# One ring of four banks for the GLA mixer's values, updates and outputs, and the output's transposes moved behind the second value

## The chip, the cores and the metric

The kernel runs on one core of one Trainium2 chip. The metric is the device time of one execution in microseconds (us), as the median of several runs. Three runs of the kernel before took 2820.91, 2823.19 and 2827.33 us.

Names used below: PE is TensorE's matmuls and PEld its weight loads, DVE is VectorE, ACT is ScalarE, POOL is GpSimd, SP is SyncE, which issues the DMAs. PSUM is the memory that matmuls write to; it has eight banks, and the stage of this change uses all eight.

## The reference

One step of a two-layer trunk on 1024 prompt frames and 32 frames of a running stream, model width 1024. Layer 0 mixes with retention, layer 1 with gated linear attention (GLA); behind each mixer stands a convolutional feed-forward part. The change concerns GLA: 4 heads, keys of 128, values of 256.

```python
def gla_chunk(S, xs):
    q, k, v, lg = xs
    b = jnp.cumsum(lg, axis=1)
    expo = b[:, :, None] - b[:, None, :]          # masked to be causal
    A = jnp.einsum('bihd,bjhd,bijhd->bhij', q, k, jnp.exp(expo))
    intra = jnp.einsum('bhij,bjhe->bihe', A, v)
    cross = jnp.einsum('bihd,bhde->bihe', q * jnp.exp(b), S)
    S_new = jnp.exp(bL)[..., None] * S + jnp.einsum('bjhd,bjhe->bhde', k * jnp.exp(bL[:, None] - b), v)
    return S_new, intra + cross
...
    o = o * lax.rsqrt(jnp.mean(o * o, axis=-1, keepdims=True) + EPS) * norm_g
    return (jax.nn.silu(r) * o) @ w_out, S
```

A frame's output is the scores A times the values, plus the decayed query times the state S; then the state is decayed and updated with keys times values. The output of each head is normalised over its 256 columns.

## The kernel before

All matmuls are fp32 by parts: each operand is split into a high part and a remainder (names ending in h and l), and three products are added in PSUM (high x high, high x low, low x high).

The 1056 frames are cut into three chunks c of 384, 384 and 288 columns, and each chunk into minors of 128 frames (the last minor of chunk 2 is the 32 sample frames). The GLA stage (`gla`, L891) runs over twelve units, one for each head h and chunk c. For a unit the code is written in this order:

- `project` of the *next* unit: gate, query and key, 49 matmuls into two banks called "pj".
- `store[0]`, that is `finish` of the *previous* unit: its last minor's `attend`, then the normalisation: DVE and ACT turn the sums of squares into a factor (L1157 to L1162) and DVE scales the output tile `oraw` (L1164).
- `scores` of this unit: many small matmuls into two banks "lv" (L1005, L1011, L1023), DVE masks (L1015, L1028) that build A, transposes of the decayed keys kd into "pj" (L1036), then the splits of A and of the keys on ACT and DVE (L1044 to L1048).
- `store[1]` of the previous unit: for each half e of the 256 output columns three transposes of `oraw` (L1170) into a bank of "pj" (e = 0) or "lv" (e = 1), one copy on ACT (L1173) and one DMA to DRAM (L1174). Only the next layer part reads it.
- `mix` of this unit: `value(0)`, `value(1)`, `attend(0)`, `value(2)`, `attend(1)`.
- `weigh` of the next unit: differences on POOL (L968, L972), exponentials on ACT (L1188) and products on DVE (L970, L974) for seven levels of the decay.

A `value` is 24 matmuls of 128x256 into a bank of tag "v" (two of them), read by ACT (vh, L1102) and DVE (vl, L1103). For the sample frames it is 16 matmuls, with vh from L259 and L260. An `attend` first splits the state (gSh on ACT L1077, gSl on DVE L1078). Then come three matmuls for the update `pu` (L1119 to L1121), read by DVE at L1124, which makes the new state gS, and six for the output `po` (L1135 to L1141), read twice by ACT: the squares (L1142) and the copy to `oraw` (L1143). `pu` and `po` share the tag "ou" with two banks.

This written order is not the order on the chip. A planner at compile time puts the instructions of each engine in one fixed queue: of those that its own costs say are ready, the one that was written earliest goes first. It also gives each tile a bank of its tag's ring. On the chip each engine works through its queue in order, and an instruction that comes to a bank that has not been read out yet waits, with all that stands behind it. So matmuls of the first value stand among the scores and the transposes today, wherever the planner held the latter not ready.

Of the kernel before, what the change touches and what calls it, by code (L numbers as in the profile page):

```python
# [9 lines left out]
F32 = mybir.dt.float32  # L10
# [6 lines left out]
P = 128  # L17
# [11 lines left out]
GH, GDK, GDV = 4, 128, 256  # L29
# [23 lines left out]
def trunk_kernel(ctx: ExitStack, tc: tile.TileContext, io):  # L53
# [3 lines left out]
    def pool(name, bufs=1, **kw):  # L57
        return tc.tile_pool(name=name, bufs=bufs, reuse_waits="tile", **kw)
# [30 lines left out]
    def uid():  # L89
        cnt[0] += 1  # L90
        return cnt[0]
# [799 lines left out]
    def gla(closers):  # L891
# [3 lines left out]
        pp = es.enter_context(pool("gps", space=PSUM))  # L895
# [8 lines left out]
        def t384(pl, tag, dt=F32, bufs=2, w=384):  # L904
            return pl.tile([P, w], dt, tag=tag, name=f"{tag}_{uid()}", bufs=bufs)
# [3 lines left out]
        def groups_of(c):  # L909
            return [(0, 3, P)] if c < 2 else [(0, 2, P), (2, 3, TS)]  # L910
# [142 lines left out]
        state = {}  # L1053
        mask = [None]

        def mix(h, c, u):
            Ah, Al, qh, ql, kh, kl, eL = u
            c0, n = CM[c]
            mins = minors(c)
            groups = groups_of(c)  # L1060
            if c == 0:
                wv[h] = [load_w(io["w_gv"][h, t]) for t in range(2)]
                if h == GH - 1:
                    preload(("w_gg", 0), ("w_gg", 1))
                state[h] = None
            if (h, c) == units[-1]:
                oraw = w_tile(f"oraw{uid()}").bitcast(F32)[:, :3 * GDV].rearrange(
                    "p (m e) -> p m e", m=3)
            else:
                oraw = g2.tile([P, 3, GDV], F32, tag="oraw", name=f"oraw{uid()}", bufs=2)  # L1070
            ss = g2.tile([P, 3, 4], F32, tag="gss", name=f"gss{uid()}", bufs=2)
            vs = {}

            def split_state(st, tag):
                sh = g2.tile([P, GDV], F32R, tag=f"gSh{tag}", name=f"gSh{uid()}", bufs=1 if tag else 2)
                sl = g2.tile([P, GDV], F32R, tag=f"gSl{tag}", name=f"gSl{uid()}", bufs=1)
                S.copy(sh, st)  # L1077
                V.tensor_tensor(sl, st, sh.bitcast(F32), op=ALU.subtract)  # L1078
                return sh, sl

            if c == 2:
                st = g2.tile([P, GDV], F32, tag="gSi", name=f"gS{uid()}")
                nc.sync.dma_start(st, io["state_gla"][h])
                s_in = st, *split_state(st, "i")

            def value(mi):
                o, t0, L = mins[mi]
                m = t0 // P
                pv = pp.tile([P, GDV], F32, tag="v", name=f"pv{uid()}", bufs=2)

                def wpart(kt):
                    ev = slice((kt % 4) * GDV, (kt % 4) * GDV + GDV)
                    return [w_[:, ev] for w_ in wv[h][kt // 4]]

                value_rows(pv, wpart, t0, xs)
                vh = g2.tile([P, GDV], F32R, tag="vh", name=f"vh{uid()}", bufs=3)
                if t0 >= TP:
                    stack_v(vh, pv)
                    vs[mi] = vh, None
                    return  # L1100
                vl = g2.tile([P, GDV], F32R, tag="vl", name=f"vl{uid()}", bufs=3)
                S.activation(vh, pv, AF.Copy, scale=rc[:, m:m + 1])  # L1102
                V.scalar_tensor_tensor(vl, pv, rc[:, m:m + 1], vh.bitcast(F32),  # L1103
                                       op0=ALU.mult, op1=ALU.subtract)
                vs[mi] = vh, vl

            def attend(mi):
                o, t0, L = mins[mi]
                vh, vl = vs[mi]
                samp = t0 >= TP  # L1110
                st = s_in[0] if samp else state[h]
                cross = st is not None
                if cross:
                    sh, sl = s_in[1:] if samp else split_state(st, "")
                pu = pp.tile([P, GDV], F32, tag="ou", name=f"ouu{uid()}", bufs=2)
                if samp:
                    PE.matmul(pu, kh[:, mi], vh, start=True, stop=True)
                else:
                    PE.matmul(pu, kh[:, mi], vh, start=True, stop=False)  # L1119
                    PE.matmul(pu, kl[:, mi], vh, start=False, stop=False)  # L1120
                    PE.matmul(pu, kh[:, mi], vl, start=False, stop=True)  # L1121
                sn = g2.tile([P, GDV], F32, tag="gS", name=f"gS{uid()}", bufs=2)
                if cross:
                    V.scalar_tensor_tensor(sn, st, eL[:, mi:mi + 1], pu, op0=ALU.mult, op1=ALU.add)  # L1124
                else:
                    S.copy(sn, pu)
                state[h] = sn
                if t0 >= TP - P:
                    dst = io["o_gla_s"] if samp else io["o_gla_p"]
                    nc.sync.dma_start(dst[h], sn)  # L1130
                po = pp.tile([P, GDV], F32, tag="ou", name=f"ou{uid()}", bufs=2)
                if samp:
                    PE.matmul(po[:L], Ah[:, mi, :L], vh, start=True, stop=False)
                else:
                    PE.matmul(po, Ah[:, mi], vh, start=True, stop=False)  # L1135
                    PE.matmul(po, Al[:, mi], vh, start=False, stop=False)
                    PE.matmul(po, Ah[:, mi], vl, start=False, stop=not cross)
                if cross:
                    PE.matmul(po[:L], qh[:, o:o + L], sh, start=False, stop=False)
                    PE.matmul(po[:L], ql[:, o:o + L], sh, start=False, stop=False)  # L1140
                    PE.matmul(po[:L], qh[:, o:o + L], sl, start=False, stop=True)  # L1141
                S.activation(oraw[:L, mi], po[:L], AF.Square, accum_out=ss[:L, mi, 0:1])  # L1142
                S.copy(oraw[:L, mi], po[:L])  # L1143

            value(0)
            value(1)
            attend(0)
            value(2)
            attend(1)

            def finish():
                attend(2)
                for m0, m1, L in groups:
                    m_ = ss[:L, m0:m1, 1]
                    r_ = ss[:L, m0:m1, 2]
                    t_ = ss[:L, m0:m1, 3]
                    V.tensor_scalar(m_, ss[:L, m0:m1, 0], 1.0 / GDV, EPS, op0=ALU.mult, op1=ALU.add)  # L1157
                    expln(t_, m_, AF.Ln)
                    expln(r_, t_, AF.Exp, scale=-0.5)
                    V.tensor_tensor(t_, r_, r_, op=ALU.mult)  # L1160
                    V.scalar_tensor_tensor(t_, t_, -0.5, m_, op0=ALU.mult, op1=ALU.mult)
                    V.scalar_tensor_tensor(r_, t_, 1.5, r_, op0=ALU.add, op1=ALU.mult)  # L1162
                    for mi in range(m0, m1):
                        V.tensor_scalar(oraw[:L, mi], oraw[:L, mi], ss[:L, mi, 2:3], None, op0=ALU.mult)  # L1164

            def store(lv, room):
                for e in range(2):
                    pt = (lv("pt") if lv else small() if e else t384(pp, "pj", w=512))[:, :3 * P].rearrange("p (m i) -> p m i", m=3)
                    for mi, (o, t0, L) in enumerate(mins):
                        PE.transpose(pt[:, mi, :L], oraw[:L, mi, e * P:e * P + P], ident[:L, :L])  # L1170
                    ot = room()
                    w = n if lv or e == 0 else 3 * P
                    S.copy(ot[:, :w], pt.rearrange("p m i -> p (m i)")[:, :w])  # L1173
                    nc.sync.dma_start(scr_o[1][2 * h + e, :, c0:c0 + n], ot[:, :n])  # L1174
            return finish, store
# [16 lines left out]
        g2 = es.enter_context(pool("g2", side="right"))  # L1192
# [22 lines left out]
        store = None  # L1215
        for i, u in enumerate(units):
            nxt = units[i + 1] if i + 1 < len(units) else None
            if nxt:
                p = project(*nxt)
            if store:  # L1220
                store[0]()
            sc = scores(*u, w)
            if store:
                store[1](None, lambda: t384(g2, "ot"))
            h, c = u
            if c == 1 and h + 1 < GH:
                for j in range(2):
                    preload(("w_gqk", h + 1, j))
                    order(last_w[1], mask[0])
            store = mix(*u, sc)  # L1230
            if nxt:
                w = weigh(*nxt, p)
        store[0]()
# [728 lines left out]
```

## Time and profile before

| | |
|---|---|
| median of three runs | 2823.19 us (2820.91 to 2827.33) |
| profiled execution, its own time | 2822.85 us |
| its span in the trace | 2820.7 us |
| TensorE matmul busy | 2748.1 us, 97% |
| VectorE, ScalarE, GpSimd busy | 74%, 47%, 10% |
| mean granted TensorE clock | 0.995 of full speed |
| the GLA units in the trace | about 1640 to 1925 us |

Times in the trace are in us from the span's start. A line of the timeline gives the start, the duration, the engine, the line of the code, the operation, the tiles (written <- read) and, in brackets, the idle time of the engine before it with what ended that. Matmuls overlap: one takes 0.28 us from start to end, and the next may start 0.12 us behind it. A list of waits gives the waiting instruction, what released it, then total us, how often, and the longest.

### The profile page before, as it was taken

The page shows a single profiled execution, that of the slowest core. Times are in us where ns is not written, and L with a number is a line of the kernel's source. Part 1 is how long each engine was busy: PE and PEld are TensorE (multiplying, and loading weights), DVE is VectorE, ACT ScalarE, POOL GpSimd, SP SyncE. Part 2 cuts the span into 40 slices and gives each one's busy share as a digit, 9 for nine tenths or more (in the row PEclk, how much of TensorE's full clock was granted, in tenths as well). Part 3 has the DMA queues.
Part 4 walks back from the last instruction along what each step waited for, and adds up shares of the span by engine and source line. Part 5 has one row for each costly group of instructions (what it writes and reads, how often), then busy time and mean ns, then how long its engine had stood idle before and what let it go on. Part 6 is the DMA issues. An engine that isn't in the chain of part 4 may idle for free.

```text
span 2820.7 us, 54472 instructions
## 1 busy us (share of the span) xinstructions
PE 2748.1 (97%) x21978; PEld 2649.3 (94%) x21978; DVE 2099.6 (74%) x3493; ACT 1322.2 (47%) x2388; POOL 273.1 (10%) x480
## 2 busy tenths in 40 slices
PE   8999999999999999999999999999999999999998
PEld 8999988878899999999999989989999999999997
DVE  7777777777577878887875687874388788878756
ACT  8433344443455544444542565653244444445434
POOL 1000000000011111111000122220021111110001
PEclk9999999999999999999999999999999999999999
DMA  6333386664866123332856511115531233328573
GB/s 223 108 121 109 107 282 204 211 194 160 273 189 219 61 84 107 137 130 84 284 194 225 186 30 53 53 45 174 170 100 62 84 107 134 134 81 284 195 237 113
DMA packets 232478, 419.48 MB, mean 149 GB/s; under 512 B 27393, under 2 KB 145793, under 8 KB 231201
## 3 DMA queue, kind: packets, MB, share of 16 engines
q1 hardware_dynamic: 231680, 415.40, 44.9%
q8 instruction: 172, 2.82, 0.4%
q14 instruction: 82, 0.66, 0.1%
q10 hardware_dynamic: 544, 0.59, 0.1%
HBM read 292.08 MB, written 123.85 MB: 147 GB/s over the span
## 4 chain that ended last, share of the span: by engine, by line
PE 80%; DVE 9%; DMA 5%; ACT 4%; issue 2%; POOL 1%; SPq 0%; DVEq 0%; ACTq 0%; POOLq 0%
PE pu L341 16%; PE pu L336 16%; PE pu L340 16%; PE pd L1316 3%; PE pd L1315 3%; PE pd L1317 3%; PE psv L242 1%; PE psv L241 1%; PE psv L240 1%; PE pj L127 1%; PE pj L128 1%; DMA raw<-w_ro 1%; PE pj L129 1%; PE pg L127 1%; PE pg L128 1%
## 5 line engine op out<-in xcount | busy, mean ns | idle before, releaser
L106 DVE TENSOR_TENSOR wlo<-raw,whi 128x1024 fp32r<-128x1024 f32 (+1 forms) x147 | 179.7, 1226 | 94.9 <-ACT whi L106 39.8
L1571 ACT COPY AR<-pu 128x264 f32<-128x264 f32 x264 | 98.8, 374 | 292.8 <-PE pu L341 290.1
L341 PE MATMUL pu<-XA,wgl 128*128 128x264 f32 x752 | 213.6, 284 | 0.0
L336 PE MATMUL pu<-XA,wgh 128*128 128x264 f32 x752 | 213.0, 283 | 0.0
L340 PE MATMUL pu<-XA,wgh 128*128 128x264 f32 x752 | 213.0, 283 | 0.0
L106 ACT CAST whi<-raw 128x1024 fp32r<-128x1024 f32 (+1 forms) x147 | 152.7, 1042 | 103.8 <-DMA raw<-w_ro 41.3
L1593 DVE SCALAR_TENSOR_TENSOR AR<-AR,cw 128x1058 f32<-128x1058 f32 x88 | 116.0, 1319 | 58.5 <-ACT AR L1592 54.0
L1315 PE MATMUL pd<-XB,whi 128*128 128x264 f32 x552 | 157.9, 286 | 1.7 <-DVE rm L212 1.7
L1317 PE MATMUL pd<-XB,wlo 128*128 128x264 f32 x552 | 157.0, 284 | 0.0
L1316 PE MATMUL pd<-XB,whi 128*128 128x264 f32 x552 | 156.7, 284 | 0.0
L336 PE MATMUL pu<-XA,wsh 128*128 128x264 f32 x520 | 148.3, 285 | 1.6 <-ACT AR L1571 0.8
L341 PE MATMUL pu<-XA,wsl 128*128 128x264 f32 x520 | 147.9, 284 | 0.8 <-DVE wsl L309 0.8
L340 PE MATMUL pu<-XA,wsh 128*128 128x264 f32 x520 | 147.2, 283 | 0.0
L1567 DVE TENSOR_TENSOR AR<-AR,pu 128x264 f32<-128x264 f32 (+2 forms) x440 | 145.1, 370 | 0.0
L309 DVE TENSOR_TENSOR wtl<-rv,wth 128x1024 fp32r<-128x1024 f32 x58 | 71.5, 1233 | 97.7 <-ACT wth L309 93.6
L336 PEld LDWEIGHTS pu<-XA,wgh 128*128 128x128 f32 x752 | 141.3, 188 | 0.0
L341 PEld LDWEIGHTS pu<-XA,wgl 128*128 128x128 f32 x752 | 141.2, 188 | 0.0
L340 PEld LDWEIGHTS pu<-XA,wgh 128*128 128x128 f32 x752 | 141.2, 188 | 0.0
L336 PE MATMUL pu<-XA,whi 128*128 128x264 f32 x448 | 127.7, 285 | 2.1 <-ACT XA L1462 1.2
L341 PE MATMUL pu<-XA,wlo 128*128 128x264 f32 x448 | 127.5, 286 | 1.5 <-DVE wlo L106 1.5
L340 PE MATMUL pu<-XA,whi 128*128 128x264 f32 x448 | 127.2, 285 | 0.5 <-DVE XA L1447 0.4
L336 PE MATMUL pu<-XA,wth 128*128 128x264 f32 x408 | 116.1, 285 | 0.7 <-ACT wth L309 0.7
(497 smaller groups left out, 10454.5 us busy)
## 6 DMA issues: line engine op xcount, KB each, us to landing
raw<-w_ro SPq DMA_DIRECT2D x52, 512.0 KB, 5.0
rg<-w_up SPq DMA_DIRECT2D x44, 512.0 KB, 3.7
rv<-w_up SPq DMA_DIRECT2D x44, 512.0 KB, 3.6
scr_h<-AR SPq DMA_DIRECT2D x44, 512.0 KB, 2.6
AR<-scr_x SPq DMA_DIRECT2D x32, 528.0 KB, 5.0
scr_x<-AR SPq DMA_DIRECT2D x32, 528.0 KB, 3.8
raw<-scr_w SPq DMA_DIRECT2D x32, 512.0 KB, 4.8
AR<-scr_h SPq DMA_DIRECT2D x28, 528.0 KB, 4.9
```

The source lines that it names most:

```text
L106: last_w[:] = S.copy(hi[:, k], raw[:, k]), V.tensor_tensor(lo[:, k], raw[:, k], hi[:, k].bitcast(F32), op=ALU.subtract)
L127: PE.matmul(ps, hi[:, k], rh, start=kt == 0, stop=False)
L309: last_w[:] = S.copy(h, src), V.tensor_tensor(l_, src, h.bitcast(F32), op=ALU.subtract)
L336: mm = PE.matmul(ps, wh[:, k], x[:, 0, kt], start=m in (1, 2, 4, 5) and kt == 0, stop=False, skip_group_check=True)
L340: PE.matmul(ps, wh[:, k], x[:, 1, kt], start=False, stop=False, skip_group_check=True)
L341: mm = PE.matmul(ps, wl[:, k], x[:, 0, kt], start=False, stop=kt == 3, skip_group_check=True)
L1315: PE.matmul(o, w[0][:, k], h[0][:, :n], start=i == 0, stop=False)
L1316: PE.matmul(o, w[0][:, k], h[1][:, :n], start=False, stop=False)
L1317: self.last_mm = PE.matmul(o, w[1][:, k], h[0][:, :n], start=False, stop=i == nk - 1)
L1567: V.tensor_tensor(u[:, d:d + n], t[:, o:o + n], b[:, o:o + n], op=op)
L1571: S.copy(t, b)
L1593: V.scalar_tensor_tensor(cj, uj[:, 1:T + 3], cw[:, nt, 1:2], cj, op0=ALU.mult, op1=ALU.add)
```

## The change

Three tile calls change their tag: the value's `pv`, the update's `pu` and the output's `po` now share one tag "vo" with four banks, in place of two tags with two banks each. In number of banks nothing changes. Each tile is asked for at the size of a full bank and cut to 256 columns.

`store[1]` of the previous unit is no longer called between `scores` and `mix`. It is handed to `mix` and called there between `value(1)` and `attend(0)`. In chunk 1 the loads of the next head's query and key weights, which are written between the two places, so come ahead of it, and in chunk 0 the loads of the value weights in `mix`. The last unit's output is transposed in the next part, as before.

```diff
-        def mix(h, c, u):
+        def mix(h, c, u, between):
...
-                pv = pp.tile([P, GDV], F32, tag="v", name=f"pv{uid()}", bufs=2)
+                pv = pp.tile([P, 512], F32, tag="vo", name=f"pv{uid()}", bufs=4)[:, :GDV]
...
-                pu = pp.tile([P, GDV], F32, tag="ou", name=f"ouu{uid()}", bufs=2)
+                pu = pp.tile([P, 512], F32, tag="vo", name=f"ouu{uid()}", bufs=4)[:, :GDV]
...
-                po = pp.tile([P, GDV], F32, tag="ou", name=f"ou{uid()}", bufs=2)
+                po = pp.tile([P, 512], F32, tag="vo", name=f"ou{uid()}", bufs=4)[:, :GDV]
...
             value(0)
             value(1)
+            if between:
+                between()
             attend(0)
             value(2)
             attend(1)
...
             sc = scores(*u, w)
-            if store:
-                store[1](None, lambda: t384(g2, "ot"))
             h, c = u
...
-            store = mix(*u, sc)
+            store = mix(*u, sc, (lambda st=store: st[1](None, lambda: t384(g2, "ot"))) if store else None)
```

## The prediction

> **What bounds the kernel now.** I read the page first.
>
> ```profile
> span 2820.7 us, 54472 instructions
> PE 2748.1 (97%) x21978; PEld 2649.3 (94%) x21978; DVE 2099.6 (74%) x3493; ACT 1322.2 (47%) x2388; POOL 273.1 (10%) x480
> ```
>
> TensorE sets the time as a whole: it is idle for 72.6 of 2820.7 us. The change touches only the GLA stage, so I then asked for the busy times of that stretch and for what TensorE waited for in it.
>
> ```profile
> 1640.00:1925.00 285.00, 270.53 (x3562) 260.07 (x3563) 222.51 (x557) 168.14 (x543) 67.50 (x83) 0.99 0.17 53
> ```
>
> Columns: stretch, its length, then busy time of PE, PEld, DVE, ACT and POOL, the granted clock, the DMA share, GB/s. TensorE is idle 14.5 us here, DVE is at 78%, ACT at 59%. Nothing else is near its limit, so what the change can win lies in these 14.5 us, in matmuls that run slower than they need, and in the clock (0.99, not 1.00).
>
> ```profile
> PE ouu L1119 <- DVE gS L1124: 3.5, 3, 1.2
> ...
> PE ou L1135 <- ACT oraw L1143: 2.0, 3, 0.7
> PE pj L1170 <- DVE oraw L1164: 1.9, 6, 0.4
> ```
>
> Three waits belong to the change, each with total, count and longest. The first two are the two-bank ring "ou": an update (pu) waits until the previous update has been added to the state, an output (po) until the previous output has been copied out. Each comes three times, in the last chunk (c = 2) of heads 0 to 2. The third is the transposes waiting for the normalised output.
>
> **The gap in chunk 2**, seen in time (head 0, instructions of PE, then ACT, then DVE):
>
> ```profile
> 1701.84 0.28 PE L246 MATMUL pv<-whi,xs 128*128 128x256 f32 x1
> 1703.31 0.36 PE L1119 MATMUL ouu<-vh,kh 128*128 128x256 f32 x1 [1.19 <-DVE gS L1124]
> 1703.51 0.28 PE L1120 MATMUL ouu<-vh,kl 128*128 128x256 f32 x1
> 1703.63 0.37 PE L1121 MATMUL ouu<-vl,kh 128*128 128x256 f32 x1
> 1704.67 0.39 PE L1135 MATMUL ou<-vh,Ah 128*128 128x256 f32 x1 [0.67 <-ACT oraw L1143]
> ```
>
> ```profile
> 1700.89 0.63 ACT L1188 ACTIVATE d<-d 128x192 f32<-128x192 f32 x2 [2.15 <-POOL d L968]
> 1702.00 0.64 ACT L1188 ACTIVATE d<-d 128x192 f32<-128x192 f32 x2 [0.47 <-POOL d L968]
> 1702.54 0.46 ACT L1102 ACTIVATE vh<-pv,rc 128x256 fp32r<-128x256 f32 x1
> ...
> 1704.24 0.37 ACT L1143 COPY oraw<-ou 128x256 f32<-128x256 f32 x1
> ```
>
> ```profile
> 1702.69 0.48 DVE L1124 SCALAR_TENSOR_TENSOR gS<-gS,eL,ouu 128x256 f32<-128x256 f32 x1
> 1703.08 0.48 DVE L1103 SCALAR_TENSOR_TENSOR vl<-pv,rc,vh 128x256 fp32r<-128x256 f32 x1
> ...
> 1703.87 0.43 DVE L1078 TENSOR_TENSOR gSl<-gS,gSh 128x256 fp32r<-128x256 f32 x1
> ```
>
> Matmuls of 128x256 that wait for nothing start 0.12 us apart (1703.51 to 1703.63). From 1701.84 to 1703.31 are 1.47 us, so 1.35 are lost before pu; from 1703.63 to 1704.67 are 1.04, so 0.92 are lost before po. ACT had been standing behind two exponentials that waited for POOL, which is why vh comes only at 1702.54.
>
> **The clock after the gap.** I laid windows over the stretches where the clock column falls:
>
> ```profile
> 1702.20:1705.62 3.42, 1.64 (x10) 1.44 (x11) 2.35 (x8) 3.21 (x10) 0.54 (x1) 1.00 0.00 0
> 1705.62:1709.03 3.41, 3.41 (x13) 3.41 (x12) 2.80 (x6) 3.41 (x10) 0.00 (x0) 0.50 0.31 61
> 1845.56:1848.98 3.42, 1.78 (x13) 1.37 (x11) 3.35 (x9) 2.74 (x10) 1.47 (x2) 1.00 0.00 0
> 1848.98:1852.39 3.41, 3.19 (x12) 3.20 (x13) 2.32 (x6) 3.41 (x9) 0.00 (x0) 0.50 0.11 12
> ...
> 1773.90:1777.30 3.40, 1.97 (x15) 1.57 (x13) 3.34 (x9) 2.69 (x10) 1.63 (x2) 1.00 0.01 2
> ```
>
> Two of the three gaps (heads 0 and 2) are followed by 3.41 us at half clock, after a stretch in which PE was busy for 1.64 and 1.78 us. Head 1's gap is as long but its busiest part fell otherwise (1.97 us) and the clock stayed. Half clock for 3.41 us costs at most 1.7 us; the second stretch has 0.2 us of idle in it, so I take 1.6 each, 3.2 in all.
>
> **The transposes.** In chunk 2 they stand together; in chunk 1 and chunk 0 they are spread among the matmuls of the first value.
>
> ```profile
> 1694.01 0.27 PE L1170 MATMUL pj<-ident,oraw 128*128 128x128 f32 x1
> ...
> 1694.58 0.36 PE L242 MATMUL pv<-whi,XA 128*128 128x256 f32 x1
> ```
>
> ```profile
> 1668.95 0.28 PE L240 MATMUL pv<-whi,XA 128*128 128x256 f32 x1
> ...
> 1670.86 0.28 PE L240 MATMUL pv<-whi,XA 128*128 128x256 f32 x1
> ```
>
> ```profile
> 1719.24 0.33 PE L1170 MATMUL pj<-ident,oraw 128*128 128x128 f32 x1
> 1719.33 0.36 PE L240 MATMUL pv<-whi,XA 128*128 128x256 f32 x1
> 1719.53 0.28 PE L241 MATMUL pv<-wlo,XA 128*128 128x256 f32 x1
> 1720.21 0.24 PE L1170 MATMUL pj<-ident,oraw 32*128 32x32 f32 x1 [0.40 <-DVE oraw L1164]
> ...
> 1720.85 0.56 PE L1170 MATMUL lv<-ident,oraw 128*128 128x128 f32 x3
> 1721.33 0.39 PE L242 MATMUL pv<-whi,XA 128*128 128x256 f32 x1
> 1721.56 0.28 PE L240 MATMUL pv<-whi,XA 128*128 128x256 f32 x1
> ```
>
> Six together take 0.57 us (1694.01 to 1694.58), 0.10 each. In chunk 1, 1.91 us hold six of them and six value matmuls: 0.60 + 0.72 = 1.32 would do, 0.59 are lost. In chunk 0, 2.32 us hold five and six (the "..." are three value matmuls): 0.50 + 0.72 = 1.22 would do, 1.10 are lost. The loss is idle time, and the slower start of a value matmul behind a transpose (0.20 instead of 0.12).
>
> **The change part by part.**
>
> No instruction is added or removed. *Transposes behind the second value* (eleven chunks; the twelfth is done in the next layer): 48 value matmuls, 5.7 us, now stand between the scores and the transposes, so the product oraw, some 0.5 us late today, is long there, and the six can stand together as in chunk 2. Worth 3 x 0.59 + 3 x 1.10 + 0, the gain where they already stand together being nothing: 5.1 us; bounds 2 (the 1.9 of the wait alone) and 6. What is late next: pu waits for kl, po for Al, but the transposes' own time still lies ahead of those. With the transposes go two copies on ACT and two stores on SP per chunk. The stores fall behind the next head's weight loads on SP; nobody in this stage reads them. The copies (0.48 us, row below) come after vh and fall into ACT's stretch before 1700.89, where 2.15 us of idle hide them; without that cover they push the exponentials and the second vh, 0.96 us in three chunks 2. I charge a third, 1.0; bounds 0 and 2.9.
>
> ```profile
> 1694.76 0.48 ACT L1173 COPY ot<-pj 128x384 f32<-128x384 f32 x1 [1.29 <-PE pj L1170]
> ```
>
> *Ring of four, po's wait.* po takes a bank that was left two tiles earlier instead of one: pu's, free at 1703.17 (gS above), before po can start at 1703.75. Its last operand gSl ends at 1704.30, and five matmuls of 0.12 cover 1703.75 to 1704.35. So 0.92 x 3 = 2.8 us; bounds 1.4 and 2.8.
>
> *Ring of four, pu's wait.* If pu's bank is free, vh still ends at 1703.00 and vl at 1703.56, and pu's third matmul needs vl: it starts at 1703.63 today. So I take 0. Lower bound: pu gets the second value's own bank and its first matmul waits for vl, 0.25 later, -0.8 in three. Upper: vh is ordered ahead of the exponentials, 1.35 x 3 = 4.0.
>
> *Clock.* Without po's 0.92 the critical stretches are busy 2.5 to 2.7 of 3.41 us, more than head 1's 1.97, which kept the clock. 3.2 us; bounds 0 and 3.2.
>
> One rule of the Trainium skill disagrees: "TensorE: Matmul & The Clock Gate", Part 1, says that the clock falls after at least one idle window of about 3.4 us. The trace has no such idle window here and the clock fell at 1.64 of 3.42 us busy, so the rows decide; by the rule the two slow stretches would have another cause and stay, and the sum would be 3.2 less.
>
> Sum: 5.1 - 1.0 + 2.8 + 0 + 3.2 = 10.1 us. The profiled execution took 2822.85 us (2.15 outside its span), 0.34 below the median 2823.19. 2822.85 - 10.1 = 2812.75; against the median **2813.1 us**.
>
> **The rivals.**
>
> *A: the gap only moves.* ACT's copies land ahead of the second vh in chunk 2 and take back 0.96 us, all of the 0.92 that po wins; the slow stretches stay. Left are the transposes: 2823.2 - 5.1 = 2818.1, no measurable change. For it: ACT is the engine that came last (1702.54). Against: the 2.15 idle ahead of it.
>
> *B: the clock stays* although the gap shrinks: 10.1 - 3.2 = 6.9, 2816.3. Against: head 1.
>
> *C: the whole gap goes*, since each second value ends 0.57 us earlier (its six transposes) and vh slips ahead of the exponentials: 4.0 and the copies' 1.0 more, 2808.
>
> *D, the slower one: the first value waits for an output.* In the shared ring the next chunk's first value may be given the bank that the previous chunk's last output has just left.
>
> ```profile
> 1690.26 0.31 PE L1005 MATMUL lv<-q,k 128*32 128x32 f32 x5
> 1692.60 0.39 PE L240 MATMUL pv<-whi,XA 128*128 128x256 f32 x1
> ```
>
> ```profile
> 1691.04 0.38 ACT L1143 COPY oraw<-ou 128x256 f32<-128x256 f32 x1
> ```
>
> That copy ends at 1691.42. Today the value starts at 1692.60, behind all scores; if the new order puts it ahead of them, at 1690.26, it waits 1.16 us, with all scores queued behind it in order and DVE's masks waiting for those. Eleven such waits are 12.8 us; with the clock's gain lost too, 2823.2 - 6.9 + 12.8 = 2829.1. It decides from 6.9 / 11 = 0.63 us a chunk. Against it: three other banks are usually older.
>
> *E: nothing moves*, because the whole order is planned anew and gains and losses cancel: 2823.
>
> **How the numbers follow.** Forecast 0.40 (its own range 2809 to 2817.5), A 0.24, B 0.08, C 0.11, D 0.12, E 0.05. This kernel's runs tell about 0.2% (5.6 us) from no change, so faster means under 2817.5. Faster: 0.37 of the forecast, 0.05 of A, 0.06 of B, all of C: 0.59. Slower: D and a little of E, 0.13. Same: 0.28. The range reaches down past C to 2806 and up through E to 2825, leaving most of D out.
>
> **What would show it.** Right: no wait of po for oraw and none of the transposes for oraw in the list of TensorE's waits; the transposes standing six together ahead of pu; no row at half clock between 1640 and 1925; PE idle there near 8 us. Wrong: vh of chunk 2 later than today relative to the last value matmul (A), half-clock rows still there (B), a wait of pv for oraw or gS (D). The forecast fails if the new order opens gaps elsewhere in the stage, above all between the scores and DVE's masks.

## The result, and the profile after

The changed kernel takes 2818.26 us (median of ten runs, 2811.38 to 2820.63) against 2824.07 us for the kernel before in the same series (ten runs, 2819.64 to 2830.73). The ratio is 0.9975 with a 95% interval of 0.9967 to 0.9983, so 7.1 us less (4.8 to 9.3). The forecast was 10.1 us less, and faster by more than 0.2%. The middle of the measurement is 0.25% faster, and its interval begins at 0.17%. The median lies inside the range of 2806 to 2825 us, but just above the forecast's own narrower one (2809 to 2817.5), and the forecast's saving of 10.1 us lies outside the measured 4.8 to 9.3.

The page of the profiled execution (2818.43 us) opens so:

```profile
span 2816.2 us, 54463 instructions
PE 2749.2 (98%) x21978; PEld 2651.5 (94%) x21978; DVE 2098.0 (74%) x3493; ACT 1320.7 (47%) x2388; POOL 266.2 (9%) x480
```

The GLA stretch of it, columns as before:

```profile
1640.00:1925.00 285.00, 277.10 (x3663) 267.04 (x3663) 223.44 (x561) 171.37 (x551) 71.67 (x85) 0.99 0.17 54
```

TensorE is idle for 7.9 us there, where it was 14.5 (the stretch now holds 101 matmuls more, since all ends earlier). The list of what it waited for:

```profile
PE lv L1023 <- issue: 1.9, 1, 1.9
PE lv L1023 <- DVE A L1015: 1.5, 4, 0.9
PE pj L127 <- DVE t L940: 1.3, 2, 1.0
PE ou L1141 <- DVE gSl L1078: 1.0, 4, 0.3
PE ouu L1119 <- DVE vl L1103: 0.6, 3, 0.2
```

The three waits of the change are gone: no update waits for the new state, no output for the copy of the last one, no transpose for the normalised output. Two small ones stand in their place, an output that waits for the split state (gSl) and an update that waits for the second value's low part (vl).

Chunk 2 of head 0, on TensorE:

```profile
1699.79 0.49 PE L1172 MATMUL pj<-ident,oraw 128*128 128x128 f32 x3
1700.12 0.49 PE L1172 MATMUL lv<-ident,oraw 128*128 128x128 f32 x3
1700.36 0.36 PE L1119 MATMUL ouu<-vh,kh 128*128 128x256 f32 x1
...
1703.30 0.28 PE L246 MATMUL pv<-whi,xs 128*128 128x256 f32 x1
1703.79 0.39 PE L1119 MATMUL ouu<-vh,kh 128*128 128x256 f32 x1 [0.21 <-DVE vl L1103]
...
1704.25 0.32 PE L1135 MATMUL ou<-vh,Ah 128*128 128x256 f32 x1
...
1704.84 0.28 PE L1140 MATMUL ou<-gSh,ql 128*128 128x256 f32 x1
1705.38 0.38 PE L1141 MATMUL ou<-gSl,qh 128*128 128x256 f32 x1 [0.26 <-DVE gSl L1078]
```

The six transposes stand together ahead of the first update (0.57 us). From the start of the third value's last matmul to the second update are 0.49 us where they were 1.47 (0.12 is the distance without a wait). The gap before the output of that update is gone, and 0.54 us lie before the output's last matmul. ACT in the same stretch:

```profile
1698.11 0.47 ACT L1102 ACTIVATE vh<-pv,rc 128x256 fp32r<-128x256 f32 x1
1698.48 0.61 ACT L1190 ACTIVATE d<-d 128x192 f32<-128x192 f32 x2
1700.32 0.62 ACT L1190 ACTIVATE d<-d 128x192 f32<-128x192 f32 x2 [1.22 <-POOL d L968]
1701.79 0.37 ACT L1190 ACTIVATE d<-d 128x192 f32<-128x192 f32 x1 [0.85 <-POOL d L968]
1702.06 0.46 ACT L1102 ACTIVATE vh<-pv,rc 128x256 fp32r<-128x256 f32 x1
1702.42 0.47 ACT L1175 COPY ot<-pj 128x384 f32<-128x384 f32 x1
1702.77 0.49 ACT L1175 COPY ot<-lv 128x384 f32<-128x384 f32 x1
1703.14 0.65 ACT L1190 ACTIVATE d<-d 128x192 f32<-128x192 f32 x2
```

In the profile of before, these two rows stand ahead of the ones at 1700.89 and 1702.00 that the prediction shows:

```profile
1697.25 0.48 ACT L1102 ACTIVATE vh<-pv,rc 128x256 fp32r<-128x256 f32 x1
1697.62 1.13 ACT L1188 ACTIVATE d<-d 128x192 f32<-128x192 f32 x4
```

The second value's vh still stands behind exponentials that wait for POOL, but behind fewer of them: between the first value's vh and the second's were eight exponentials, now there are five. So vh ends 2.85 us after the last matmul of its value starts (1699.67 to 1702.52); before it was 4.05 (1698.95 to 1703.00). The output copies come behind it.

To see where the time went, I took from the timelines the starts of each unit's gate matmul (L936), which begins the projection behind a unit, and the differences between them. The units are (head, chunk); the last interval runs to the last output matmul. Unit (0,0), which has no transposes in it, takes 24.74 us both before and after and is left out. Two of the runs described below are in the table already.

| interval, us | before | changed | ring alone | move alone |
|---|---|---|---|---|
| (0,1) | 22.32 | 21.80 | 22.31 | 21.81 |
| (0,2) | 24.99 | 23.71 | 24.21 | 24.43 |
| (1,0) | 25.71 | 23.71 | 24.18 | 24.13 |
| (1,1) | 22.35 | 22.31 | 22.29 | 21.79 |
| (1,2) | 24.97 | 23.71 | 24.07 | 24.44 |
| (2,0) | 24.20 | 23.76 | 24.20 | 24.18 |
| (2,1) | 22.32 | 21.79 | 22.32 | 21.80 |
| (2,2) | 25.61 | 23.71 | 24.09 | 24.45 |
| (3,0) | 24.96 | 24.36 | 24.93 | 24.17 |
| (3,1) and (3,2) | 40.02 | 40.56 | 38.44 | 41.44 |
| sum | 257.45 | 249.42 | 251.04 | 252.64 |

So the units are 8.0 us shorter. The rest of the span is 3.5 us longer (2820.7 - 257.45 = 2563.3 before, 2816.2 - 249.42 = 2566.8 after): 1.9 us of that lie ahead of the first interval, although TensorE's order is the same up to the start of GLA, and 1.6 behind the last. Much of it is the clock in places that the change doesn't touch. These two stretches of the changed kernel are at half clock for 6.83 us each, where the profile of before has 3.41 us each (a mean of 0.75 over the same two windows):

```profile
69.82:76.65 6.83, 6.04 (x28) 5.93 (x28) 6.06 (x8) 4.47 (x6) 0.00 (x0) 0.50 0.50 149
762.73:769.56 6.83, 5.05 (x23) 5.05 (x24) 6.21 (x13) 4.68 (x12) 1.50 (x2) 0.50 0.84 238
```

One more stretch of 3.41 us at half clock is found in the profile of before alone (first row), and one behind GLA in the changed kernel alone (second row):

```profile
1459.85:1463.26 3.41, 3.41 (x17) 3.41 (x18) 2.87 (x4) 0.84 (x2) 0.00 (x0) 0.50 0.84 299
2660.55:2663.96 3.41, 3.41 (x18) 3.41 (x17) 3.41 (x5) 1.45 (x2) 0.00 (x0) 0.50 0.26 107
```

A last one of the changed kernel, at 1636.55, falls into unit (0,0), which is no longer for it. On balance the changed kernel's profile so has one stretch more that counts ahead of the units and one more behind them, at most 1.7 us each. The single pair of profiles therefore shows 4.4 us less, and the timed runs, which average over such differences, 7.1.

### The profile page after: what moved, and what is told of

Read it like the earlier page. It is cut to its first block, busy times and chain, and to the rows that moved or that the text cites. A ratio compares the mean times of both kernels' runs of the same rounds, so it can differ in the third digit from the quotient of the medians.

```text
span 2816.2 us, 54463 instructions
## 1 busy us (share of the span) xinstructions
PE 2749.2 (98%) x21978; PEld 2651.5 (94%) x21978; DVE 2098.0 (74%) x3493; ACT 1320.7 (47%) x2388; POOL 266.2 (9%) x480
## 4 chain that ended last, share of the span: by engine, by line
PE 79%; DVE 9%; DMA 5%; ACT 4%; issue 2%; POOL 1%; SPq 0%; DVEq 0%; ACTq 0%; POOLq 0%
PE pu L341 16%; PE pu L336 16%; PE pu L340 16%; PE pd L1315 3%; PE pd L1316 3%; PE pd L1317 3%; PE psv L242 2%; PE psv L241 2%; PE psv L240 2%; PE pj L127 1%; PE pj L128 1%; PE pj L129 1%; PE pg L127 1%; PE pg L128 1%; PE pg L129 1%
```

## The experiments

Each was timed in five rounds beside the kernel before on the same chip.

**The ring alone.** The diff's three tile lines, `store[1]` left between `scores` and `mix`.

> The ring of four alone; the transposes stay between the scores and the first value. Theory 1 (the ring takes away only po's wait, and the move fills pu's wait, since it puts the six transposes, 0.57 us, behind the second value, where PE waits for vh): pu's gap in chunk 2 stays at 1.35 us or grows by 0.25, because pu's bank is the second value's; po's 0.92 goes, 0.4 of it coming back as a wait for gSl; the transposes stay spread (0.6 and 1.1 us lost in chunks 1 and 0). So 1 us less than the kernel before, and up to 3 more if the half-clock stretches go. Theory 2 (the terms as forecast: the ring is worth po's 2.8 us and the clock's 3.2): 6 us less, no half-clock stretch in the GLA units.

Measured: ratio 0.9984 (0.9974 to 0.9995), 4.5 us less. Waits of TensorE in the GLA stretch, and the windows over chunk 2 of the three heads:

```profile
PE ouu L1119 <- DVE gS L1124: 3.6, 3, 1.3
PE pj L1170 <- DVE oraw L1164: 1.9, 6, 0.4
```

```profile
1702.31:1705.73 3.42, 2.24 (x20) 2.04 (x18) 2.31 (x8) 1.61 (x6) 2.76 (x3) 1.00 0.00 0
1705.73:1709.14 3.41, 3.27 (x21) 3.27 (x22) 2.33 (x5) 3.38 (x8) 0.00 (x0) 1.00 0.00 0
1773.99:1777.41 3.42, 2.31 (x19) 2.09 (x17) 3.35 (x9) 2.73 (x10) 1.61 (x2) 1.00 0.01 2
1845.67:1849.09 3.42, 2.23 (x16) 2.08 (x15) 2.54 (x8) 3.19 (x9) 0.55 (x1) 1.00 0.00 0
```

The ring takes away po's wait and nothing of pu's: that one is 3.6 us in three places, as before (3.5). By the lists it waits for the new state here and for vl in the changed kernel, so the planner seems to hand out another bank in each. That decides for theory 1 on pu. The 0.4 us that theory 1 had coming back as a wait for gSl did not come. The time doesn't decide: 4.5 lies between the 4 of theory 1 with the clock and the 6 of theory 2, and its interval (1.4 to 7.3) holds both. The clock's share came with po's wait alone: the stretches are busy 2.2 to 2.3 us and keep the clock. Chunk 2 without any clock effect, head 1: 24.97 to 24.07, 0.9 us.

**The move alone.** The changed kernel with the tags "v" and "ou", two banks each.

> The move alone; two rings of two banks as in the kernel before. Theory 1: the transposes stand together (3 us), pu's gap in chunk 2 shrinks from 1.35 to about 0.7 us (2 us in three), po's wait for oraw stays, and the half-clock stretches go or not by where the clock's windows fall: 5 to 8 us less than the kernel before. Theory 2: 5 us less by the transposes, pu's gap and po's wait as before, half-clock stretches as before.

Measured: ratio 0.9992 (0.9982 to 1.0001), 2.3 us less; from 0.3 more to 5.1 less. Its waits:

```profile
PE ou L1135 <- ACT oraw L1143: 2.6, 6, 0.7
...
PE ouu L1119 <- DVE gS L1124: 2.0, 3, 0.7
```

That is less than either theory had it (5 to 8 and 5), though the interval just reaches 5; the units of its profile are 4.8 us shorter. pu's wait falls from 1.2 to 0.7 us each, with the old ring: the six transposes behind the second value fill time in which TensorE waited for vh. po's wait stays, and comes in six places instead of three. The ring's 4.5 and the move's 2.3 add up to 6.8, close to the 7.1 of both, though each is known to some 3 us only. In head 1's chunk 2 they are 0.90 and 0.53, together 1.43, and both at once win 1.26.

**Three banks.** The changed kernel with `bufs=3` for the shared tag.

> The changed kernel with three banks in the ring instead of four. In ring order the third value gets the second value's bank and has to wait for its vh and vl, which end some 1.6 us after the third value starts in the changed kernel. If the bank at the right moment is what the ring of four buys: the wait of pv for vl appears in chunk 2, 1.5 us or more each, half-clock stretches come back, and the time is 5 to 12 us above the changed kernel. If four banks do no more than three (the move is the whole gain): within 2 us of the changed kernel.

Measured: ratio 1.0039 (1.0024 to 1.0053), 11 us slower than before and some 18 slower than the changed kernel, more than the 5 to 12 expected.

```profile
PE pv L240 <- DVE vl L1103: 8.6, 7, 2.3
PE pv L246 <- DVE vl L1103: 6.3, 3, 2.1
```

```profile
1724.14:1727.55 3.41, 1.08 (x9) 0.88 (x9) 2.60 (x7) 2.96 (x11) 0.71 (x2) 1.00 0.13 40
1727.55:1730.97 3.42, 3.42 (x18) 3.42 (x18) 0.42 (x1) 0.30 (x2) 0.00 (x0) 0.50 0.16 54
```

A value now waits for the value before it, 14.9 us in ten places, in chunks 0 and 1 too, and half-clock stretches follow (four in the units). This is close to rival D, the slower one: a value waits for a bank, though for the value before it (vl) and not for an output's copy. With four banks no such wait is in the lists.

**Transposes behind the third value.**

```diff
-            if between:
-                between()
             attend(0)
             value(2)
+            if between:
+                between()
             attend(1)
```

> The changed kernel with the transposes behind the third value, ahead of the second attend, instead of behind the second. Theory 1: what matters in chunk 2 is 0.57 us of PE work anywhere between the second value and the second update, so the update starts at the same time, and only the short waits for gSl may go: within 2 us of the changed kernel. If the place right behind the second value matters (the copies on ACT come late and hold the state's split): 2 to 5 us above it, with a longer wait of po for gSl.

Measured: ratio 0.9989 (0.9979 to 0.9999), 3 us less than before, 4 more than the changed kernel. Chunk 2 is 0.85 us shorter there (22.86 and 22.83 in heads 1 and 2, against 23.71), but the unit behind it is 2.1 us longer there, by a wait that neither theory named:

```profile
PE pj L127 <- ACT ot L1175: 5.7, 4, 1.6
```

One half of the transposes goes into a bank of "pj", the projection of the next unit needs that bank, and ACT's copy out of it now comes too late.

**The same, both halves in the "lv" banks** (`pt = small()` for both).

> Transposes behind the third value in every chunk, as in the run before, but both halves in the lv banks, so that no pj bank waits for the copies on ACT. If the wait of the next unit's projection for that copy (5.7 us in four places) is what spoiled the place behind the third value: that wait is gone, chunk 2's units stay at 22.9 us (23.7 in the changed kernel) and the time is 1 to 3 us below the changed kernel. If the place itself costs (the state's split behind the copies on ACT): still 2 us or more above the changed kernel, with another wait in its stead.

Measured: ratio 0.9976 (0.9967 to 0.9985), level with the changed kernel. The wait for the copies is gone, and chunk 2 is shorter still (22.69). But chunk 0 gives back about 1 us (24.69 and 24.79 against 23.71 and 23.76): the projection starts earlier and its key now waits for the gate's bank (list of waits: pj for t of L940, 2.7 us in four places). So neither side of the expectation came.

**Only chunk 2 behind the third value.** Transposes of a store in chunk 2 there, both halves in "lv"; chunks 0 and 1 as in the changed kernel.

> Only chunk 2 has its transposes behind the third value, there with both halves in the lv banks; chunks 0 and 1 as in the changed kernel. By the first theory for the third value: chunk 2's units 0.8 us shorter in three heads, 2 to 3 us below the changed kernel. By the rival: the same time as the changed kernel or above, with the saving of chunk 2 lost in the unit behind it.

Measured: 2813.35 us, ratio 0.9965 (0.9951 to 0.9978). Chunk 2 is 22.69, chunk 0 is 24.45 and 24.47: 1.0 us won and 0.7 given back, as the rival said for the unit behind. Run again beside the changed kernel:

> The same kernel as in the run with chunk 2 alone, beside the changed kernel on one chip. If the shorter chunk 2 is a gain: 2 to 4 us below the changed kernel in the medians of the same call. If its units' gain is paid back behind them: within 1 us.

> The changed kernel itself, in the same call. It should stand 0.2 to 0.3% below the kernel before; the half-clock stretches of its profile should again fall outside chunk 2, wherever the clock's windows fall.

Measured: 2813.43 us, ratio 0.9966 (0.9954 to 0.9978), against 2816.46 us and 0.9973 (0.9963 to 0.9982) for the changed kernel, which again has no half-clock stretch in a chunk 2. It has the lowest median of all, twice, by 3 us in this call; the two intervals overlap, and the units explain only 3 x (1.0 - 0.7), so 1 us of it. That it beats the kernel before is shown; that it beats the changed one is likely, but not shown.

**The copies twice.** Each output copy on ACT (L1175) done a second time.

> The changed kernel with each of the two output copies on ACT done twice: 0.96 us more work on ACT in each of eleven chunks. If these copies are hidden behind ACT's waits for POOL: within 1 us of the changed kernel, the GLA units as long as there. If they stand in chunk 2's chain (the charge of 1.0 us in the forecast's sum): chunk 2's units 0.5 to 1 us longer, 2 to 3 us in all, and up to two half-clock stretches more.

Measured: 2816.8 us, ratio 0.9973 (0.9962 to 0.9984), level with the changed kernel. Chunk 2 takes 23.55, not longer than 23.71: there the copies stand behind vh and are hidden. (It is even shorter, because gSl takes 0.42 us here and 0.72 in the changed kernel, though it starts 0.13 later.) Chunk 0 takes 24.55 and 24.63, 0.85 longer, so in that chunk there is no such cover.

**Control: both halves in "lv", at the changed kernel's place.**

> Control for the lv banks: the changed kernel, its transposes at their place, both halves in the lv banks. By either theory no wait of the projection for the copies exists there, so within 1 us of the changed kernel; if the scores' matmuls now wait for the copies to free an lv bank, a wait of lv for ot shows up and the units grow by as much.

Measured: 2815.31 us, ratio 0.9968 (0.9957 to 0.998). No wait of lv for the copies; (1,0), (1,2) and (2,0) within 0.02 us of the changed kernel. The bank of the transposes makes no difference by itself.

**The gate behind query and key,** on top of chunk 2's version, so that the key needn't wait for the gate's bank.

```diff
-            b = gate(h, c)
-            return b, *qk_out(c, qk_products(h, c))
+            qk = qk_out(c, qk_products(h, c))
+            return gate(h, c), *qk
```

> Chunk 2's transposes behind the third value (as in the run with chunk 2 alone), and the next unit's gate behind its query and key instead of ahead of them, so that the key's matmuls don't wait for the gate's bank. If that wait (4.2 us in four places there) is only the bank: it goes and the time falls by 1 to 2 us against the run with chunk 2 alone. If the gate's chain (exponential, logarithm, scan, then POOL's differences) is what the next scores wait for: it starts some 7 us later and a wait of the scores for DVE takes the place, same time or longer.

Measured: ratio 0.9995 (0.9987 to 1.0004), the gain is lost, as the second expectation had it. The key's wait is gone, and others take its place:

```profile
PE lv L1023 <- DVE A L1015: 2.7, 7, 0.5
PE ou L1141 <- DVE gSl L1078: 2.5, 3, 0.8
PE ouu L1119 <- DVE vl L1103: 2.2, 6, 0.4
```

That a gate that starts later puts the whole chain of decays, and with it DVE's other work, later fits these waits; no run shows it separately.

## Why the prediction was right

Sign and bound were right; the size was 10.1 and came out at 7.1. The number alone would not have told the forecast from two of its rivals: A had 5.1 us less and B 6.9, both inside the measured 4.8 to 9.3. What speaks for the forecast's mechanism are the waits: those of po and of the transposes for oraw are gone, the six transposes stand together, and PE is idle for 7.9 us. One of its signs failed: the changed kernel's profile has a half-clock row between 1640 and 1925, though not in a chunk 2.

The units of the trace allow a check of each term. I take the clock's share out first: (1,0) and (2,0) do the same work, and before the first, which holds a half-clock stretch, took 25.71 against 24.20, so 1.51; (2,2) and (3,0) share the second stretch, 25.61 - 24.97 = 0.64 and 24.96 - 24.20 = 0.76, so 1.40. (The ring alone has 24.93 in (3,0) without a slow stretch; there the key waits for the gate's bank, 0.52 us idle.)

*The transposes* were put at 5.1 us and brought 1.9: chunks 1 won 0.52, 0.04 and 0.53, chunks 0 won 0.49, 0.44 and, with a new wait for the gate in (3,0) (0.33 us), -0.16. This is the term that was mis-sized. In chunk 1 the 0.59 forecast came in two of three heads; in the third the wait for gSl took it. In the second execution of the changed kernel, (1,1) takes 21.81 and (0,1) and (2,1) 22.31: the same half microsecond comes and goes per execution, while the ring alone and the kernel before have 22.3 in all three heads. In chunk 0 the forecast let six transposes take 0.60 us because they do so in chunk 2. They don't there:

```profile
1793.23 0.55 PE L1172 MATMUL pj<-ident,oraw 128*128 128x128 f32 x3
1793.71 0.61 PE L1172 MATMUL lv<-ident,oraw 128*128 128x128 f32 x3
1794.26 0.38 PE L1119 MATMUL ouu<-vh,kh 128*128 128x256 f32 x1
```

Six in one row, two of which handle the 32 sample frames, take 1.03 us. So some 0.4 of the 1.10 was never to be had, and the row of three in the profile of before (1720.85 to 1721.33, 0.48) had shown it. Why the remaining 0.7 came to 0.49 and 0.44 only stays open.

*po's wait*: 0.92 us in each chunk 2, forecast in full, with gSl hidden by 0.05. It went, but gSl comes 0.54 - 0.12 = 0.42 late. DVE shows what came ahead of it:

```profile
1703.26 0.47 DVE L1103 SCALAR_TENSOR_TENSOR vl<-pv,rc,vh 128x256 fp32r<-128x256 f32 x1
1703.66 0.47 DVE L1124 SCALAR_TENSOR_TENSOR gS<-gS,eL,ouu 128x256 f32<-128x256 f32 x1
...
1704.60 0.72 DVE L1078 TENSOR_TENSOR gSl<-gS,gSh 128x256 fp32r<-128x256 f32 x1
```

vl now goes ahead of the new state gS, which starts 0.13 us before the update (1703.66 and 1703.79) where it started 0.62 before it (1702.69 and 1703.31). The forecast had left DVE's order as it was. Also, gSl itself takes 0.72 us where it took 0.43 (1703.87), in all three chunks 2; why, no run shows.

*pu's wait* was put at 0, because its third matmul needs vl. That premise held: in the changed kernel pu waits for vl, the bank being the second value's, as the lower bound had it. The sum missed two things. The moved transposes are themselves work that fills this gap: from the second value's last matmul to the third's are 3.63 us (1699.67 to 1703.30), where they were 2.89. The run with the move alone shows that this shortens the wait (1.2 to 0.7 us). And the update did not come later for it, but 0.24 earlier: 4.12 us behind the second value's last matmul (1703.79) where it was 4.36 (1703.31). Here a part of rival C came true, which had vh slipping ahead of the exponentials and the whole gap going. vh slipped ahead of three of eight exponentials, in the changed kernel and with the move alone, and not with the ring alone. So vl ends 4.06 us behind that matmul where it ended 4.61; as the update of the changed kernel waits for vl, without this it would start some 0.5 us later (an estimate from these times; no run separates it from the filling). Why the planner moved vh, no run shows.

*The copies on ACT*, charged with 1.0 in chunk 2, cost nothing there: doubled, they lengthen no chunk 2. With all three, chunk 2 won 1.28, 1.26 and 1.90 - 0.64 = 1.26, so 3.8 us against 2.8 - 1.0 = 1.8 forecast: 0.92 - 0.42 = 0.50 of each from po's wait and 1.47 - 0.49 = 0.98 from pu's gap, less 0.2 lost in later starts elsewhere in the unit.

*The clock* was put at 3.2. Both stretches went, 2.9 us by the units. But in the changed kernel's profile another one opened at 1882, behind a stall of 1.9 us before the scores of (3,1) that the profile can't name ("issue"); before, such a stall (1.5 us) left the clock alone.

```profile
1878.89:1882.30 3.41, 1.54 (x55) 1.43 (x43) 2.26 (x10) 0.67 (x3) 0.90 (x1) 1.00 0.02 5
1882.30:1885.72 3.42, 3.42 (x19) 3.42 (x18) 3.01 (x8) 1.55 (x6) 1.61 (x2) 0.50 0.00 0
```

The sum over the units: 1.9 + 3.8 + 2.9 - 0.5 (the last interval, with this stretch in it) = 8.1, against 8.0 in the table. That the sum came this near to 10.1 is in part luck: the transposes brought 3.2 less than forecast, and chunk 2, where pu's wait was put at nothing, 2.0 more.

Rival A (the gap only moves) falls with the doubled copies, and with vh, which ends earlier behind its value and not later; B (the clock stays) falls with the windows of the ring alone. C came in part, as told above. D, the wait of a value for a bank, is real, but at three banks. E, an order planned anew that cancels the gains, was seen only mildly: the "pj" wait in (3,0) and gSl's.

## What to carry to other kernels

A ring's size is read from what its next tile waits for, not from the number of tiles alive: two times two banks and one times four are the same memory, and the shared one removed a wait, while three banks made ten new ones. Work that is moved to cover one wait is worth most where it also fills another gap: look at both ends of the move. Before costing a group of small matmuls by its cheapest instance, find the row of the very shape.

## What the runs showed of the hardware

In the GLA stage the clock falls for one stretch of 3.41 us after a stretch of 3.41 us with about half of it idle. The boundaries lie on a grid within an execution: in the profile of before the two slow stretches start 42 times 3.413 us apart (1705.62 and 1848.98). In the GLA units of the profiles of all kernels told of here, sixteen stretches were followed by half clock: PE was busy in them for 0.91 to 1.92 of 3.41 us. Of those at 2.0 us or more none was. Between 1.60 and 1.99 both happened: 1.63, 1.68, 1.78 and 1.92 lost the clock; 1.84 and 1.87 (twice each), 1.86, 1.89, 1.93 and 1.99 kept it, and so did 1.60 once, at the stage's start. (A window cut a hundredth otherwise moves these figures by as much: 1.63 and 1.99 are the 1.64 and 1.97 of the prediction's rows.) Just ahead of these units, where TensorE waits once for 1.5 us in twelve of the thirteen profiles, a stretch busy for 1.88 or 1.89 us lost the clock in five profiles and kept it in three. That the edge isn't sharp may come from the modelled ends of the matmuls; no run tells. The Trainium skill, "TensorE: Matmul & The Clock Gate", Part 1, gives a free-running window of 3413 ns, which agrees with the length of 3.41 us; its condition of a whole idle window does not agree with 1.78 us busy and half clock behind it. So idle time of 1.5 to 2 us costs itself and, when it happens to fall into one such stretch, it can cost 1.4 to 1.5 us more. This can also make one execution differ from the next: the same kernel's two profiles have the unnamed stall of 1.9 us in both, with half clock behind it in one alone.
